# A four-layer hybrid backbone on one core: where the low halves of the weights are formed, and two edits in the Mamba-2 layer

## The chip, the cores and the metric

The kernel runs on one core of a Trainium2 chip. The metric is the device time of one execution, in microseconds (us), as the median of several runs. A core has TensorE (matmuls, "PE"; its weight loads are "PEld"), VectorE ("DVE"), ScalarE ("ACT"), GpSimd ("POOL") and SyncE ("SP"), which here only issues transfers. Each engine works through its own queue in order; the transfers (DMA) run beside them.

## The reference, cut to what matters

One inference step of a diffusion backbone: 128 context tokens and 512 latent tokens of width 1024 pass four layers, each with another token mixer: a bidirectional Mamba-2 SSD, a gated MLP, an S5 state-space layer with a GLU, and neighbourhood attention. Every layer projects into the mixer and out of it again:

```python
for i in range(DEPTH):                      # 4 layers
    hc, gate_c = adaln(xc, norm_g[i], cond_ctx @ w_mod[i] + b_mod[i])
    hl, gate_l = adaln(xl, norm_g[i], cond_lat @ w_mod[i] + b_mod[i])
    yc, yl = mixer_i(hc @ w_in), mixer_i(hl @ w_in)
    xc = xc + gate_c * (yc @ w_out[i])
    xl = xl + gate_l * (yl @ w_out[i])
```

In the SSD layer (32 heads in 8 groups of 4, chunks of 128 tokens) the result is the sum of a part within each chunk and a part from the state that enters the chunk, forward and backward:

```python
y_diag = einsum('bclgn,bcsgn,bgrcls,bcsgrp->bclgrp', cm, bm, decay_in, xd)
y_off  = einsum('bclgn,bcgrpn,bgrcl->bclgrp', cm, states, exp(a_cum))
y = y_diag + y_off
```

## The kernel before

The 640 tokens lie along the free axis, the channels on the 128 partitions. A big product runs as three matmuls of reduced-width fp32 (fp32r) pieces: each operand is split into a high half (`hi`, the value rounded) and a low half (`lo`, what rounding lost), and hi·hi + hi·lo + lo·hi is summed in PSUM. A *unit* is a weight block of 1024 x 128: it comes by one 512 KB transfer into a `raw` buffer (two of them), and `unit` makes `whi` and `wlo` of it (three buffers each). There are 289 units: 65 in the SSD layer with its output projection, 64 in the MLP layer, 80 in the S5 layer (32 in, 32 GLU, 16 out), 80 in the attention layer.

`unit` makes the halves so: ScalarE copies raw into `whi` (L223), ScalarE writes minus raw, rounded, into `wlo` (L224), and a transfer that GpSimd issues adds raw to `wlo` (L225). The raw buffer comes free when that transfer has ended. The older helper `split` (L201 to L204) instead subtracts hi from the source on an engine; `N.wlo` names that engine (VectorE, or GpSimd in the output projections and the attention layer), and `N.wlos` is a pattern of engines that the S5 layer sets and that `turn_over` clears. In the kernel before `unit` computes the engine and doesn't use it.

`stream` plays the units on TensorE in *slots*. A slot is one k-tile of one unit: 128 rows of the contraction, six matmuls of 320 columns. A unit is eight slots. While unit i - 1 has its first slot, unit i is made. Each layer gives `play` a table `at` of other work by slot. TensorE's order is written out by hand that way; in the SSD and the attention layer the order of the other engines and of SP's transfers is a planner's, in the S5 layer with its GLU those of VectorE, ScalarE and GpSimd are by hand too, as is the end of each output projection (from slot 112 on).

In the SSD layer each of the 8 groups has its table from a start slot t (52, 92, 132, 180, 228, ...): for the chunks, in the order 0, 1, 4, 2, 3 and 9 slots apart, `decay` (the matrix W by scans on VectorE), `turn` (transposes, products) and 9 slots later `diag` (the part of y within the chunk). The state goes through three steps j = 1 to 3: `fade` (GpSimd: H times a decay, into a new H buffer of three), `advance` (TensorE `st`, VectorE adds it to the new H) and 6 slots after it `off` (TensorE: H times C into PSUM; VectorE: times `eab`, which has a single buffer that `begin` fills for the next group; GpSimd or, in the last group, VectorE: added to y). `off` of j = 0 is at t + 7, of j = 1 to 3 at t + 24, t + 36 and t + 43. Four PSUM banks are shared by all of this. `diag` forms two products of 128 x 256, of which only the blocks of matching heads are used, and adds them to y in two steps of 64 partitions (L1061).

In the attention layer each pair of heads takes 32 slots for its weights q, k, v, z. `k` writes the split k into `K` by eight transfers from SP (L1965), and the first `scores` of the pair (L2048) reads it nine slots later. `scores` is followed by a softmax on VectorE and ScalarE (L2054 to L2059, L2059 scales e), and `turn` transposes e six slots later (L2071).

Of the kernel before, what the change touches and what calls it, by code (L numbers as in the profile page):

```python
# [9 lines left out]
AF = mybir.ActivationFunctionType  # L10
OP = mybir.AluOpType
# [19 lines left out]
TA, TY, TS, TG, TB = 6, 9, 6, 12, 6  # L31
# [86 lines left out]
class Net:  # L118
    def __init__(self, ctx, tc, I, O, layers):
        self.layers = layers  # L120
        self.ctx, self.tc, self.nc, self.I, self.O = ctx, tc, tc.nc, I, O
        nc = self.nc
        pool = lambda name, bufs=1, **k: ctx.enter_context(tc.tile_pool(name=name, bufs=bufs, **k))
        self.const = pool("const")
        self.ap = pool("act")
        self.wp = pool("wts")
        self.hp = pool("h")
        self.ps = pool("ps", space=PSUM)
        self.dr = pool("dr", space=DRAM)
        self.uid = 0  # L130
        c = self.const
        cm = c.tile([128, 136], F32, name="cmat")
        nc.sync.dma_start(cm, I["consts"][:, 0:136])
        self.ident = cm[:, 0:128]
        self.blk = cm[:, 128:136]
        self.ones = c.tile([128, 128], F32, name="ones")
        nc.vector.memset(self.ones, 1.0)
        self.eps = c.tile([128, 1], F32, name="eps")
        nc.vector.memset(self.eps, EPS)
        self.vec = c.tile([128, NVEC], F32, name="vec")  # L140
        nc.sync.dma_start(self.vec, I["vecs"])
        self.mods = {}
        self.beside = []
        self.late = []
        self.hs = []
        self.xd = I["x"]
        self.rest = False
        self.cut_in = None
        self.ready = []
        self.entry = {}  # L150
        self.nrow = NROW
        self.wlo = nc.vector
        self.wlos = ""


    def n(self, s):
# [60 lines left out]
    def unit(self, raw, m=128):  # L217
        hi, lo = (self.wp.tile([128, 8, m], F32R, tag=s, bufs=NHL, name=self.n(s)) for s in ("whi", "wlo"))
        e = self.wlo
        if self.wlos:  # L220
            e, self.wlos = {"p": self.nc.gpsimd, "v": self.nc.vector}[self.wlos[0]], self.wlos[1:] + self.wlos[0]
        nc = self.nc
        nc.scalar.copy(hi, raw)  # L223
        nc.scalar.activation(lo, raw, AF.Copy, scale=-1.0)  # L224
        nc.gpsimd.dma_start(lo, raw, accum_op=OP.add)  # L225
        return hi, lo

    def gemm(self, units, h, m=128):
# [490 lines left out]
    def put(self, yd, k, y):  # L719

        self.nc.sync.dma_start(yd[:, 2 * k:2 * k + 2, :], y)
# [62 lines left out]
class Ssd:  # L784
# [124 lines left out]
    def run(self, N, h):  # L909
        nc, I, tp = N.nc, N.I, N.tp  # L910
        self.pads = [tp.tile([128, 648], F32, name=f"pad{i}") for i in range(2)]
        self.pi = 0
        for t in self.pads:
            for a, b in ((0, 2), (130, 134), (646, 648)):
                nc.vector.memset(t[:, a:b], 0.0)
        W = I["w_ssd"]
        self.ssum = N.ssum()
        self.yd = N.dr.tile([128, 16, T], F32, name="yd0")
        N.put_beside()
        G = [{"g": g} for g in range(8)]  # L920
        jobs = []
        at = {}
        put = lambda s, f, *a: at.setdefault(s, []).append(lambda: f(*a))
        one = lambda w, f, *a: jobs.append(([W[w]], h, 128, lambda p: f(N, *a, p)))

        def tables(p):
            self.tab = self.tables(N, p)
        jobs.append(([I["w_dt"]], h, 64, tables))
        for s in range(5):
            put(TB * s + 8, lambda: next(self.tab))  # L930
        for g in range(8):
            for n, w in (("b", 32 + g), ("c", 40 + g), ("x0", 16 + 2 * g), ("x1", 17 + 2 * g)):
                one(w, self.conv, G[g], n, w - 16)
            for j in range(2 if g else 0):
                one(2 * g - 2 + j, self.gate, G[g - 1], j)

            t = 8 + 32 * (g + 1) + 16 * max(g - 1, 0) + TG + 8 * (g == 1)
            P = G[g]
            put(t - 2, self.begin, N, P)
            for i, c in enumerate((0, 1, 4, 2, 3)):  # L940
                put(t + TA * i - 8, self.decay, N, P, c)
                put(t + TA * i, self.turn, N, P, c)
                put(t + TA * i + TY, self.diag, N, P, c)
            put(t + 5, self.context, N, P)
            for j, s in enumerate((1, 2 * TA + TS, 4 * TA + TS, 4 * TA + 2 * TS + 1)):
                if j:
                    put(t + s - 3, self.fade, N, P, j)
                    put(t + s, self.advance, N, P, j)
                put(t + s + TS, self.off, N, P, j)
            for s in range(2):  # L950
                put(t + 16 * s, N.tick, 1)
        for j in range(2):
            one(14 + j, self.gate, G[7], j)
        N.play(jobs, at, after=[I["w_out"][0, 0, 0]])
        return self.yd, self.ssum
# [36 lines left out]
    def begin(self, N, P):  # L992

        nc, I, tp = N.nc, N.I, N.tp
        g = P["g"]
        P["H"] = self.t512(N, "H", 3)
        nc.sync.dma_start(P["H"], I["state_ssd"][:, g, :])
        P["eab"] = tp.tile([128, 2, 2, 512], F32, tag="eab", bufs=1, name=N.n("eab"))
        for k in range(2):
            nc.sync.dma_start(P["eab"][64 * k:64 * k + 64], self.ead[k, g][None].to_broadcast([64, 2, 2, 512]))  # L1000
# [48 lines left out]
    def diag(self, N, P, c):  # L1049

        nc = N.nc
        y, w = P["y"], P["W", c]
        py = N.bank("yd")
        for j in range(2):
            nc.tensor.matmul(py[:, 256 * j:256 * j + 256], P["xw", c][0][:, 128 * j:128 * j + 128], w[:, 256 * j:256 * j + 256],
                             start=True, stop=True)
        pv = py.rearrange("p (j h l) -> p j h l", j=2, h=2)
        for k in range(2):
            r = slice(64 * k, 64 * k + 64)
            o = y[r, :, 128 * c:128 * c + 128]  # L1060
            nc.vector.tensor_tensor(o, o, pv[r, :, k, :], op=OP.add)  # L1061

    def states(self, N, P, p, cf, cb):
        for d, c in ((0, cf), (1, cb)):
# [20 lines left out]
    def advance(self, N, P, j):  # L1085

        nc = N.nc
        Hn = P["Hn"]
        p = N.bank("st")
        self.states(N, P, p, j, 5 - j)  # L1090
        nc.vector.tensor_tensor(Hn, Hn, p, op=OP.add)
        P["H"] = Hn

    def off(self, N, P, j):

        nc = N.nc
        y, H = P["y"], P["H"]
        po = N.bank("off")
        for r in range(2):
            for d in range(2):  # L1100
                c = 1 + j if d == 0 else 4 - j
# [6 lines left out]
        for d in range(2):  # L1108
            c = 1 + j if d == 0 else 4 - j
# [472 lines left out]
class S5:  # L1582
# [80 lines left out]
    def turn_over(self, N, own, out):  # L1663
        own.close()
        out.enter_context(N.phase("glu"))
        N.nrow = 3
        N.wlos = ""

    def gate(self, N, k, p):
        z = self.tile(N, [128, T], "r3", 3)  # L1670
# [605 lines left out]
```

## Time and profile before

| | |
|---|---|
| time, median of 3 runs | 3116.27 us (3109.17 to 3117.82) |
| the profiled execution | 3107.51 us |
| its span, first to last instruction | 3105.7 us |
| TensorE busy, matmuls | 2776.5 us (89%) |
| VectorE, ScalarE, GpSimd busy | 1951.8 us (63%), 1595.9 us (51%), 1141.1 us (37%) |
| mean granted TensorE clock | 0.946 |
| transfers issued by SP, by GpSimd | 44.3% and 25.8% of 16 DMA engines' span |

The busy time tells which engine has little room; idle time of an engine that isn't the bound costs nothing. What sets the end is read from TensorE's idle time and from what ended each stretch of it. Layer by layer TensorE is in the SSD layer from about 60 us to 622, in its output projection to 760, in the MLP layer to 1340 with its output, in the S5 layer to 1885, the GLU to about 2140, its output projection to 2275, in the attention layer to 2950 and in the last projection to 3095.

### The profile page before, as it was taken

The page shows a single profiled execution, that of the slowest core. Times are in us where ns is not written, and L with a number is a line of the kernel's source. Part 1 is how long each engine was busy: PE and PEld are TensorE (multiplying, and loading weights), DVE is VectorE, ACT ScalarE, POOL GpSimd, SP SyncE. Part 2 cuts the span into 40 slices and gives each one's busy share as a digit, 9 for nine tenths or more (in the row PEclk, how much of TensorE's full clock was granted, in tenths as well). Part 3 has the DMA queues.
Part 4 walks back from the last instruction along what each step waited for, and adds up shares of the span by engine and source line. Part 5 has one row for each costly group of instructions (what it writes and reads, how often), then busy time and mean ns, then how long its engine had stood idle before and what let it go on. Part 6 is the DMA issues. An engine that isn't in the chain of part 4 may idle for free.

```text
span 3105.7 us, 50460 instructions
## 1 busy us (share of the span) xinstructions
PE 2776.5 (89%) x18252; PEld 2681.8 (86%) x18252; DVE 1951.8 (63%) x4958; ACT 1595.9 (51%) x2648; POOL 1141.1 (37%) x1482
## 2 busy tenths in 40 slices
PE   6888889899899998998889777998999999999988
PEld 3788889889899898988889777998989999999988
DVE  5987766675689888728887951006645656655732
ACT  4533444434444444265666454555356676666742
POOL 4467656412476672123453532332121111111110
PEclk8899999999999999999898898999999999999999
DMA  7666666687676677967767578667867766677575
GB/s 251 176 172 175 163 168 172 179 261 209 177 211 188 184 209 235 265 187 187 190 176 210 139 169 198 157 156 224 244 162 175 181 162 157 178 177 176 147 229 139
DMA packets 289736, 583.47 MB, mean 188 GB/s; under 512 B 79888, under 2 KB 148944, under 8 KB 288464
## 3 DMA queue, kind: packets, MB, share of 16 engines
q1 hardware_dynamic: 247424, 427.66, 44.3%
q0 software_dynamic: 42064, 152.59, 25.8%
q8 instruction: 145, 2.38, 0.3%
q14 instruction: 103, 0.84, 0.1%
HBM read 333.83 MB, written 65.70 MB: 129 GB/s over the span
## 4 chain that ended last, share of the span: by engine, by line
PE 33%; DMA 19%; DVE 12%; issue 8%; ACT 5%; POOL 3%; SPq 3%; POOLq 0%; DVEq 0%; ACTq 0%
PE acc L317 25%; DMA wlo<-raw 7%; DMA K<-k 3%; DVE S L1756 3%; DMA raw<-in_w_glu_dram 2%; DMA raw<-in_w_out_dram 2%; DVE sl L1753 2%; PE S L2048 1%; PE PT L2071 1%; SPq L1965 1%; ACT zr L1604 1%; SPq L1824 1%; PE av L2083 1%; ACT wlo L224 1%; ACT whi L223 1%
## 5 line engine op out<-in xcount | busy, mean ns | idle before, releaser
L317 PE MATMUL acc<-hhi,whi 128*128 128x320 f32 (+2 forms) x3472 | 865.9, 329 | 18.8 <-ACT hhi L203 8.5
L317 PE MATMUL acc<-hhi,wlo 128*128 128x320 f32 (+2 forms) x3472 | 827.9, 318 | 54.6 <-DMA wlo<-raw 54.1
L317 PE MATMUL acc<-hlo,whi 128*128 128x320 f32 (+2 forms) x3472 | 826.0, 317 | 3.2 <-DVE hlo L569 1.8
L225 POOL DMA_DIRECT2D wlo<-raw x289 | 253.8, 881 | 1135.1 <-ACT wlo L224 826.4
L317 PEld LDWEIGHTS acc<-hhi,wlo 128*128 128x128 f32 (+1 forms) x3472 | 600.9, 194 | 66.3 <-DMA wlo<-raw 64.8
L317 PEld LDWEIGHTS acc<-hhi,whi 128*128 128x128 f32 (+1 forms) x3472 | 602.9, 196 | 29.5 <-ACT hhi L203 14.0
L317 PEld LDWEIGHTS acc<-hlo,whi 128*128 128x128 f32 (+1 forms) x3472 | 605.0, 195 | 7.8 <-DVE hlo L569 4.2
L223 ACT CAST whi<-raw 128x1024 fp32r<-128x1024 f32 (+1 forms) x289 | 302.3, 1046 | 524.0 <-DMA raw<-in_w_out_dram 167.9
L224 ACT ACTIVATE wlo<-raw 128x1024 fp32r<-128x1024 f32 (+1 forms) x289 | 305.1, 1056 | 0.0
L429 DVE SCALAR_TENSOR_TENSOR wacc<-wm,conds,wacc 128x512 f32<-128x512 f32 x280 | 204.2, 787 | 21.6 <-DMA wm<-in_w_mod_dram 21.2
L317 PE MATMUL acc<-y,whi 128*128 128x320 f32 (+2 forms) x1024 | 203.0, 315 | 6.9 <-ACT y L203 3.4
L1756 DVE TENSOR_TENSOR S<-S,sl 128x32 f32<-128x32 f32 x1008 | 179.1, 232 | 0.0
L317 PEld LDWEIGHTS acc<-y,whi 128*128 128x128 f32 x1024 | 164.2, 191 | 10.7 <-ACT y L203 4.2
L1871 DVE TENSOR_TENSOR y<-y,sg 128x640 f32<-128x640 f32 x16 | 13.2, 825 | 202.5 <-ACT sg L1870 202.5
L905 DVE SCALAR_TENSOR_TENSOR cacc<-pad,vec,cacc 128x644 f32<-128x644 f32 x128 | 136.4, 1066 | 4.7 <-ACT cacc L903 3.0
L317 PE MATMUL acc<-y,wlo 128*128 128x320 f32 (+2 forms) x512 | 123.8, 313 | 11.2 <-DMA wlo<-raw 11.2
L2048 PE MATMUL S<-K,q 128*128 128x384 f32 (+1 forms) x320 | 91.2, 367 | 38.7 <-DMA K<-k 38.5
L2090 DVE TENSOR_TENSOR yn<-yn,av 64x128 f32<-64x128 f32 x320 | 90.4, 283 | 56.2 <-ACT yn L2088 48.5
L2007 POOL TENSOR_TENSOR yn<-yn,zn 128x128 f32<-128x128 f32 x80 | 36.5, 461 | 239.9 <-DVE yn L2090 123.5
L1753 DVE TENSOR_TENSOR sl<-S,A 128x64 f32<-128x64 f32 x504 | 119.3, 277 | 0.0
L1012 POOL TENSOR_TENSOR dd<-cmat,dt 128x512 f32<-128x512 f32 x80 | 107.7, 1353 | 15.3 <-DVE dt L816 9.7
L317 PE MATMUL acc<-gyh,wlo 128*128 128x320 f32 x384 | 94.6, 325 | 16.3 <-DMA wlo<-raw 16.3
(404 smaller groups left out, 5371.3 us busy)
## 6 DMA issues: line engine op xcount, KB each, us to landing
wlo<-raw POOLq DMA_DIRECT2D x288, 512.0 KB, 5.4
wm<-in_w_mod_dram SPq DMA_DIRECT2D x96, 512.0 KB, 6.5
raw<-in_w_out_dram SPq DMA_DIRECT2D x64, 512.0 KB, 3.9
raw<-in_w_nat_dram SPq DMA_DIRECT2D x64, 512.0 KB, 4.1
raw<-in_w_ssd_dram SPq DMA_DIRECT2D x48, 512.0 KB, 3.6
raw<-in_w_mlp_dram SPq DMA_DIRECT2D x48, 512.0 KB, 4.1
fb<-fd SPq DMA_DIRECT2D x40, 512.0 KB, 5.5
s5X<-s5gx SPq DMA_DIRECT2D x32, 512.0 KB, 5.5
```

The costliest lines, as they stand in the source:

```text
L223: nc.scalar.copy(hi, raw)
L224: nc.scalar.activation(lo, raw, AF.Copy, scale=-1.0)
L225: nc.gpsimd.dma_start(lo, raw, accum_op=OP.add)
L317: mm(p[:m, o:o + c], w[:, j, :], v(hx), start=(k == 0 and wi == 0), stop=(k == 8 * len(units) - 1 and wi == 2))
L429: e.scalar_tensor_tensor(acc[:, c], w[:, j], a, acc[:, c], op0=OP.mult, op1=OP.add)
L905: nc.vector.scalar_tensor_tensor(acc, pad[:, j:j + 644], w(j), acc, op0=OP.mult, op1=OP.add)
L1012: nc.gpsimd.tensor_tensor(dg.rearrange("p (h l) -> p h l", h=4), N.ident[:, None, :].to_broadcast([128, 4, 128]), self.dt[:, c, 32 * d + 4 ...
L1753: e.tensor_tensor(t[d], F[:, d, at[d], None, :].to_broadcast([128, 2, 32]), A[:, :, d], op=OP.mult)
L1756: e.tensor_tensor(dst[d], dst[d], t[d][:, k].rearrange("p (r g) -> p r g", r=2)[:, ::1 - 2 * k], op=OP.add)
L2007: N.nc.gpsimd.tensor_tensor(y[:, o], y[:, o], P["z"][:, o], op=OP.mult)
L2048: nc.tensor.matmul(p[:, :n], P["q"][:, hh, 128 * b:128 * b + 128], K[:, hh, i, c:c + n], start=(i == 0), stop=(i == 1))
L2090: nc.vector.tensor_tensor(y[r, o], y[r, o], p[r, w:w + 128], op=OP.add)
```

## The change

Three edits. First, `unit` has two ways. With `adds` true (the start) it forms the low half by the adding transfer as before, but in another order: negation, transfer, then the copy into `whi`. With `adds` false it calls `split`, and the engine that `N.wlo` names subtracts. `turn_over`, played at slot 270 of the S5 layer, sets `adds` false, so the units made from then on (most of the GLU's, the third output projection, the attention layer and the last projection) are split by subtraction: 30 on VectorE and 95 on GpSimd; 164 stay with the transfer. Second, `off` of j = 1 to 3 stands four slots later, and it reads the state kept for its own j. Third, `diag` forms its part of y by heads, in four products of 64 x 128 that land on the partitions where y has that head, and adds all with one step.

```diff
     def unit(self, raw, m=128):
-        nc.scalar.copy(hi, raw)
-        nc.scalar.activation(lo, raw, AF.Copy, scale=-1.0)
-        nc.gpsimd.dma_start(lo, raw, accum_op=OP.add)
+        if self.adds:
+
+            self.nc.scalar.activation(lo, raw, AF.Copy, scale=-1.0)
+            self.nc.gpsimd.dma_start(lo, raw, accum_op=OP.add)
+            self.nc.scalar.copy(hi, raw)
+        else:
+            self.split(raw, hi, lo, lo_eng=e)
         return hi, lo
...
-                put(t + s + TS, self.off, N, P, j)
+                put(t + s + TS + (4 if j else 0), self.off, N, P, j)
...
     def diag(self, N, P, c):
         py = N.bank("yd")
+
         for j in range(2):
-            nc.tensor.matmul(py[:, 256 * j:256 * j + 256], P["xw", c][0][:, 128 * j:128 * j + 128], w[:, 256 * j:256 * j + 256],
-                             start=True, stop=True)
-        pv = py.rearrange("p (j h l) -> p j h l", j=2, h=2)
-        for k in range(2):
-            r = slice(64 * k, 64 * k + 64)
-            o = y[r, :, 128 * c:128 * c + 128]
-            nc.vector.tensor_tensor(o, o, pv[r, :, k, :], op=OP.add)
+            for k in range(2):
+                h = 2 * j + k
+                nc.tensor.matmul(py[64 * k:64 * k + 64, 128 * j:128 * j + 128], P["xw", c][0][:, 64 * h:64 * h + 64],
+                                 w[:, 128 * h:128 * h + 128], start=True, stop=True)
+        o = y[:, :, 128 * c:128 * c + 128]
+        nc.vector.tensor_tensor(o, o, py[:, 0:256].rearrange("p (j l) -> p j l", j=2), op=OP.add)
...
-        P["H"] = Hn
+        P["H"] = P["H", j] = Hn
...
-        y, H = P["y"], P["H"]
+        y, H = P["y"], P["H", j]
...
         N.wlos = ""
+        N.adds = False
```

## Rows read from the trace of the kernel before

**Rows 1.** Windows: start:end, us, busy of PE, PEld, DVE, ACT, POOL; PEclk, DMA, GB/s.

```profile
55.00:622.00 567.00, 491.13 (x3108) 473.85 (x3109) 419.44 (x509) 246.58 (x391) 328.90 (x268) 0.93 0.68 173
...
2275.00:2950.00 675.00, 630.96 (x4276) 622.47 (x4275) 406.44 (x1362) 464.81 (x1023) 129.60 (x214) 0.96 0.69 172
```

**Rows 2.** Waits of TensorE over the span: waiting line, releaser, us, times, longest.

```profile
PE acc L317 <- DMA wlo<-raw: 88.1, 48, 8.6
PE off L1102 <- DVE H L1091: 43.1, 13, 6.1
PE S L2048 <- DMA K<-k: 38.5, 15, 4.1
```

**Rows 3.** Timeline of TensorE, SSD layer: start, us, line, operands, records [idle before].

```profile
189.21 2.04 PE L1102 MATMUL off<-c,H 128*128 128x128 f32 x8 [6.07 <-DVE H L1091]
192.65 1.91 PE L1067 MATMUL st<-xw,xb 128*128 128x256 f32 x4
...
301.33 0.46 PE L317 MATMUL acc<-hhi,whi 128*128 128x320 f32 x2
...
302.21 0.46 PE L317 MATMUL acc<-hhi,whi 128*128 128x320 f32 x2
...
438.69 1.13 PE L1102 MATMUL off<-c,H 128*128 128x128 f32 x8 [2.96 <-DVE H L1091]
440.54 1.02 PE L1067 MATMUL st<-xw,xb 128*128 128x256 f32 x4
```

**Rows 4.** The instructions of diag: duration ns min/median/max, first and last start, shape.

```profile
L1055 PE MATMUL yd<-dd,xb x160: 378/379/634, 136.1 to 625.1; 128*128 128x256 f32 x160
L1061 DVE TENSOR_TENSOR y<-y,yd x80: 383/419/426, 142.2 to 626.0; 64x256 f32<-64x256 f32 x80
```

**Rows 5.** Waits of TensorE for low halves: 760:1200, 1885:2140, 2140:2280, 2950:3095, in order.

```profile
PE acc L317 <- DMA wlo<-raw: 26.6, 17, 4.2
...
PE acc L317 <- DMA wlo<-raw: 16.6, 15, 1.3
...
PE acc L317 <- DMA wlo<-raw: 6.6, 2, 6.4
...
PE acc L317 <- DMA wlo<-raw: 5.3, 1, 5.3
```

**Rows 6.** Negation (ns min/median/max), and transfers: count, KB, us to landing.

```profile
L224 ACT ACTIVATE wlo<-raw x289: 625/1055/1084, 41.0 to 3068.8; 128x1024 fp32r<-128x1024 f32 x144, 128x512 fp32r<-128x512 f32 x1
...
wlo<-raw POOLq DMA_DIRECT2D x288, 512.0 KB, 5.4
...
eab<-ead SPq DMA_DIRECT2D x16, 512.0 KB, 6.5
```

**Rows 7.** Timelines of SP's queue and of TensorE, attention layer.

```profile
2382.94 0.33 SPq L214 DMA_DIRECT2D raw<-in_w_nat_dram  x1
...
2384.33 8.51 SPq L1965 DMA_DIRECT2D K<-k  x8
...
2393.46 0.48 PE L2048 MATMUL S<-K,q 128*128 128x256 f32 x2 [2.52 <-DMA K<-k]
...
2561.73 0.77 PE L2048 MATMUL S<-K,q 128*128 128x256 f32 x2 [3.81 <-DMA K<-k]
```

**Rows 8.** Groups by form, GpSimd: shape, count, busy us, mean ns, idle before.

```profile
L204 POOL TENSOR_TENSOR K<-ckv,K 128x256 fp32r<-128x256 f32 x16 | 11.7, 731 | 24.4 <-ACT K L203 24.4
...
L204 POOL TENSOR_TENSOR vT<-ckv,vT 128x128 fp32r<-128x128 f32 x16 | 7.4, 461 | 72.2 <-ACT vT L203 72.2
```

**Rows 9.** Timelines of VectorE, GpSimd and TensorE, attention layer.

```profile
2596.75 0.41 DVE L2059 TENSOR_SCALAR e<-e,mx 128x384 f32<-128x384 f32 x1
...
2599.66 0.49 PE L2071 MATMUL PT<-cmat,e 128*128 128x128 f32 x3
...
2892.67 0.73 POOL L204 TENSOR_TENSOR K<-ckv,K 128x256 fp32r<-128x256 f32 x1 [3.56 <-ACT K L203]
...
2892.72 0.90 DVE L2059 TENSOR_SCALAR e<-e,mx 128x384 f32<-128x384 f32 x1
```

More of the change, by code (lines that the diff above doesn't have):

```diff
@@ L153, in __init__ @@
         self.wlos = ""
+        self.adds = True
     def n(self, s):
@@ L221, in unit @@
             e, self.wlos = {"p": self.nc.gpsimd, "v": self.nc.vector}[self.wlos[0]], self.wlos[1:] + self.wlos[0]
-        nc = self.nc
-        nc.scalar.copy(hi, raw)
-        nc.scalar.activation(lo, raw, AF.Copy, scale=-1.0)
-        nc.gpsimd.dma_start(lo, raw, accum_op=OP.add)
+        if self.adds:
[4 more added lines that the diff above has]
+            self.split(raw, hi, lo, lo_eng=e)
         return hi, lo
@@ L995, in begin @@
         g = P["g"]
-        P["H"] = self.t512(N, "H", 3)
+        P["H"] = P["H", 0] = self.t512(N, "H", 3)
         nc.sync.dma_start(P["H"], I["state_ssd"][:, g, :])
```

## The prediction, made before the changed kernel was run

> **What bounds the kernel now.** Three views, in this order. The busy time by stretch says which engine each layer leans on: in the first layer TensorE is busy 491 of 567 us, VectorE 419 and GpSimd 329; in the attention layer TensorE is busy 631 of 675, VectorE 406 and GpSimd only 130 [rows 1]. So TensorE is the bound and only its idle time counts: VectorE, the next, still has a quarter of the first layer free. TensorE's waits, summed, then say what ends that idle time: 88.1 us in 48 waits for the low half of a weight, 43.1 us in 13 waits of an `off` matmul for the state H, 38.5 us in 15 waits of the attention scores for the transfers of K [rows 2]. The three make 170 us, and the change touches all three. The timeline last, for what stands around one wait. It also shows a price beyond the wait itself: after the 6.07 us wait at 189.21 the same `off` group took 2.04 us and its successor 1.91, where after the 2.96 us wait at 438.69 they took 1.13 and 1.02 [rows 3]. There TensorE ran at the lower of its two clock levels, 1.2 instead of 2.4 GHz (granted over the layer: 0.93 [rows 1]). From `off` to `st` it cost 3.44 against 1.85 us, and 0.9 more in `st`: 2.5 us a spell. The sum is made against the profiled execution: 3105.7 us of span, 3107.5 us in all, 8.8 below the median of the runs (3116.3). I take the sum off 3107.5 and add the 8.8 at the end.
>
> **Part 1: `off` of j = 1 to 3 four slots later.** A slot is one k-tile of the weight stream: three pairs of matmuls, 301.33 to 302.21, 0.88 us [rows 3]. Four slots are 3.52 us of TensorE work put between advance (where VectorE gets its sums) and the matmul that reads H. A wait shrinks by up to that. Ten of the 13 vanish; the three above 3.52 (6.07, the first of them [rows 3], 5.17 and 4.93) leave 2.55, 1.65 and 1.41. So 43.1 - 5.6 = 37.5 us. Five `off` groups took 2.04 or 2.05 us as that at 189.21 did; five spells at 2.5 give 12.5. Together 50. Against it: H now sits on VectorE behind its convolutions, and a TensorE that no longer waits gets ahead, so H, the weights W or a free one of the four PSUM banks are late next. Also, `eab` has one buffer: its reload waits for `off`(3), and lands 6.5 us after its issue [rows 6]. In the first two groups `off`(3) and the next group's `off`(0) now fall into one slot (52 + 47 = 92 + 7), where four lay between; the sum of that `off`(0) holds a bank for as long. Bounds 0 and 2 x 6.5 = 13. SP is held by that reload too, 3.5 us longer, with raw weight loads behind it; with the transfers at 0.68 of their time [rows 1] and 567 us for 49 weights I cost that at nothing, and at the same 13 if the cover is gone. I take 8 off: **42**, bounds 10 and 50.
>
> **Part 2: y by heads.** Two matmuls of 256 columns become four of 128 columns and 64 output rows. In the trace an fp32 matmul is two records; 40 chunks give 160 records of 256 columns [rows 4], afterwards 320 of 128. Eight records of 128 columns (`off`, 438.69) are no longer than four of 256, so in a row the four cost about the same; 0.1 us more a chunk if the gaps open gives +4 us. VectorE loses 40 of 80 additions of 0.42 us [rows 4], 17 us off its queue and not on TensorE's path. The trace has no two matmuls on the two halves of the output rows. If halves ran side by side, 0.43 of 0.85 us a chunk would go, 17 us. I take **0**, by the row nearest in shape, ends +4 and -17. The Trainium skill, "TensorEngine Tiling (Array Packing)", section "Tiling Modes", says that tiles of 64 columns load and multiply in parallel, and that changing the mode drains the engine. No row of this kernel shows either; by the first half alone the sum would be 17 better.
>
> **Part 3: the low half first, where transfers still add** (164 of 289 weights). Negation and copy on ScalarE swap. The negation takes 1.05 us, the transfer 5.4 from its issue [rows 6]; the low half comes 1.05 sooner, the copy 1.05 later, and the copy is needed some 0.6 us ahead of it but is ready about 4 earlier, so the transfer covers it. TensorE waits in these layers 88.1 - 16.6 - 6.6 - 5.3 = 59.6 us in 30 waits; 17 of them, 26.6 us, in the second layer [rows 5]. Cutting each by at most 1.05 gives 27 of the 59.6. Some of it moves to whatever is next late: **16**, bounds -10 (the copy slips behind other work of ScalarE) and 30. GpSimd waits 1.05 less at each issue, and everything queued there gains.
>
> **Part 4: 125 weights by subtraction.** `turn_over` is played at slot 270, when weight 34 has been made: 30 subtractions on VectorE in the GLU, 95 on GpSimd after it. Gone are a negation on ScalarE, an issue and 5.4 us of transfer each; raw is released at the end of the subtraction. Price on GpSimd: 0.46 us for 128 columns and 0.73 for 256, so 2.1 ns a column and 2.34 us for 1024 [rows 8]. From raw's copy the low half needs 2.34 instead of 1.05 + 5.4 = 6.45 us, 4.1 sooner. That covers all 15 waits of the GLU (16.6 us, none over 1.3), and 4.1 each of the 6.4 and 5.3 us at the two later ones [rows 5]: 24.8. Both are as long as that at 189.21 nearly, so I count a slow spell for each: +5. **29**, bounds 16 and 33. Behind a waiting subtraction on GpSimd stand the gates of yn and the splits of the cached keys; the issue it replaces waited longer there, for the negation.
>
> **Part 5: K.** K's first transfer left at 2384.33, right behind a raw load that SP had held until 2382.94 for a low half's transfer; K's eight took 8.51 us to issue, and the scores began at 2393.46, 2.52 late [rows 7]. An earlier release sends the raw load before that, and no 512 KB addition competes. The first is worth about 1 us a pair, the second is open. The wait is 38.5 / 15 = 2.6 a pair; about five pairs also have a slow spell as at 2561.73 (0.77 against 0.48 us) [rows 7]: 10 more. Bounds 0 (the planner orders SP so that the raw load still goes first) and 48. I take **28**.
>
> **Part 6: the new work on GpSimd.** About 63 subtractions of 2.34 us in the attention layer, less as many issues, raise GpSimd from 130 to some 220 of 675 us. They can hold up VectorE. At 2892.67 GpSimd's split ran 0.73 us, and VectorE's scaling of e, begun at 2892.72, took 0.90 instead of 0.41 to 0.42 [rows 9]. It waited for GpSimd's end. The scaling at 2596.75 ended 2.5 us ahead of its transposition at 2599.66 [rows 9]. So a hold of up to 2.34 is just covered; without that cover 63 x a fifth x 1.2 us = 15. I take **-5**, bounds -20 and 0. The Trainium skill, "SBUF — State Buffer", section "Who interferes with whom", states such a rule: whoever is first keeps the shared ports for a whole instruction. The trace agrees (0.90 against 0.42).
>
> **Sum.** 42 + 0 + 16 + 29 + 28 - 5 = 110. 3107.5 - 110 = 2997.5, and 8.8 more: **3006 us**.
>
> **Rivals.** *K stays late.* SP is ordered by a planner; if the raw load still leaves right before K, or K's eight issues are the limit, part 5 gives nothing: 3034. For it: the eight issues alone fill 8.5 us. Against: the raw load did wait for a transfer that is gone. *The wait for H only moves.* If the planner puts H correspondingly later on VectorE, or TensorE waits for banks, part 1 gives 10: 3038. For it: VectorE is busy 74% there. Against: H has a fixed place behind work that TensorE's slots pace. With both, 3066. *The low half doesn't come sooner*, since planned work gets between: part 3 gives nothing, 3022, inside the range. *Slower: GpSimd holds VectorE where TensorE needs it.* The 95 subtractions, mostly in the attention softmax, hold scalings and the splits behind them; at a full 2.34 us each on TensorE's path 222 us are lost against 42 + 16 + 29 = 87 gained without K: 3251. It is slower than before from 87 / 95 = 0.92 us a subtraction on. Against it: 2.5 us of slack. *Better.* The two halves of y run side by side and K's waits and all spells go: 17 + 20 more, 2969.
>
> **How the numbers follow.** Forecast (2985 to 3030) 0.47; K late 0.17; H only moves 0.11; both 0.06; better 0.09; GpSimd in the way 0.10. The likeliest is 3006. The range reaches from below the better case, with all upper bounds, to beyond both shortfalls together: 2955 to 3080; about 0.1 is left out above and 0.05 below. About 0.3% is what a measurement of this kernel can tell from no change. Faster 0.88; same 0.04 (a third of both shortfalls, a fifth of the GpSimd case); slower 0.08, the rest of that case.
>
> **What would show it.** Right: the wait of `off` for H under 10 us; no wait for a low half's transfer after some 1900 us of the before's time; raw loads in the attention layer no longer held by such a transfer; the scores' wait for K under 15 us; 95 subtractions at 2.3 to 2.5 us on GpSimd and 30 on VectorE; 40 additions of y. Wrong: a new large wait of transpositions for e or pt, `off` waiting as before, K's wait unchanged.

## The result, and the profile of the changed kernel

| | before | after |
|---|---|---|
| median | 3116.65 us (3109.17 to 3117.82) | 3027.93 us (3021.86 to 3036.23) |
| ratio after / before, 95% interval | | 0.9733 (0.971 to 0.9757) |
| profiled execution: time, span | 3107.51, 3105.7 us | 3021.86, 3020.1 us |
| mean granted clock of TensorE | 0.946 | 0.954 |

The change makes the kernel 2.7% faster: 88.7 us between the medians, 85.7 between the profiled executions. The forecast was 110 us and 3006; the time lies in its range, 22 us above it. The sum came out nearly right, its terms did not: by themselves one is about a fifth of what was forecast, one is nothing, and one is larger by two fifths.

Where the gain lies is read from when TensorE first and last uses low halves of each kind of weight (`y`: first and last projection, `yhi`: the second projection, `gyh`: the GLU and the third projection, `hhi`: the four layers' own). Up to the first projection 16.1 us are gained (625.9 to 609.8), up to the end of the second layer's projection 21.7 in all, up to the first weight of the GLU 20.9. GLU and third projection bring it to 36.5 (2273.7 to 2237.2), the attention layer to 80.8 (2961.6 to 2880.8), the last projection to 85.9. So the attention layer alone gives 44.3 us, the first layer 16.1, GLU and third projection 15.6. These compare one execution of each kernel. Among the other kernels of this study, code that is unchanged in the attention layer took 674.7 to 688.1 us there (687.9 before) and the change's own 643.3 to 645.6 (643.6 after); for GLU and third projection it is 383.5 to 390.1 and 362.0 to 369.8. The attention layer's gain is thus 29 to 45 us, that of GLU and third projection 14 to 28.

TensorE's waits over the span, of after: waiting line, releaser, us in total, times, longest. They answer to [rows 2].

```profile
PE acc L321 <- DMA wlo<-raw: 43.2, 25, 6.6
...
PE off L1106 <- DVE H L1095: 3.4, 7, 0.6
...
PE S L2053 <- DMA K<-k: 2.0, 1, 2.0
```

All three waits fell, by 121 us together, and the time fell by 86. The rest went into other waits. Most stand in the first layer; the same view of after, 38 to 606 us:

```profile
PE st L1071 <- DVE xw L1041: 12.3, 5, 3.3
PE xbT L1037 <- ACT x L910: 9.5, 6, 1.9
PE stc L1071 <- DVE xw L1041: 9.2, 3, 6.7
...
PE st L1071 <- DVE off L1110: 5.7, 2, 2.9
PE G L1048 <- DVE y L1065: 3.7, 1, 3.7
PE xbT L1037 <- DVE dd L1051: 3.5, 2, 1.9
```

These six add up to 43.9 us; in the kernel before the same six add up to 4.5. The operations themselves, after, against [rows 4], [rows 6] and [rows 8]: name and operands, count, ns min/median/max or busy us and mean ns.

```profile
L1065 DVE TENSOR_TENSOR y<-y,yd x40: 387/407/422, 142.9 to 610.3; 128x256 f32<-128x256 f32 x40
...
L205 POOL TENSOR_TENSOR wlo<-raw,whi 128x1024 fp32r<-128x1024 f32 x95 | 244.8, 2578 | 308.9 <-ACT whi L204 295.8 <-DVE mx L2061 7.7 <-POOL vT L205 3.1
...
L205 DVE TENSOR_TENSOR wlo<-raw,whi 128x1024 fp32r<-128x1024 f32 x30 | 35.5, 1221 | 0.6
```

Counts are as forecast (40 additions of y, 95 subtractions on GpSimd, 30 on VectorE), and a GpSimd subtraction has a mean of 2.58 us against an estimate of 2.34.

### The profile page after: what moved, and what is told of

The parts are those of the page before. It is cut to its first block, busy times and chain, and to the rows that moved or that the text cites. A ratio compares the mean times of both kernels' runs of the same rounds, so it can differ in the third digit from the quotient of the medians.

```text
span 3020.1 us, 50547 instructions
## 1 busy us (share of the span) xinstructions
PE 2750.9 (91%) x18412; PEld 2643.5 (88%) x18412; DVE 2051.4 (68%) x4948; ACT 1472.4 (49%) x2523; POOL 1265.0 (42%) x1452
## 5 line engine op out<-in xcount | busy, mean ns | idle before, releaser
L321 PE MATMUL acc<-hhi,wlo 128*128 128x320 f32 (+2 forms) x3472 | 824.2, 317 | 37.7 <-DMA wlo<-raw 36.4
L205 POOL TENSOR_TENSOR wlo<-raw,whi 128x1024 fp32r<-128x1024 f32 x95 | 244.8, 2578 | 308.9 <-ACT whi L204 295.8
L226 POOL DMA_DIRECT2D wlo<-raw x164 | 145.9, 895 | 540.4 <-ACT wlo L225 497.8
L227 ACT CAST whi<-raw 128x1024 fp32r<-128x1024 f32 (+1 forms) x164 | 170.4, 1039 | 227.5 <-DMA raw<-in_w_mlp_dram 75.4
L225 ACT ACTIVATE wlo<-raw 128x1024 fp32r<-128x1024 f32 (+1 forms) x164 | 173.0, 1056 | 143.0 <-DMA raw<-in_w_mlp_dram 80.9
L433 DVE SCALAR_TENSOR_TENSOR wacc<-wm,conds,wacc 128x512 f32<-128x512 f32 x280 | 222.6, 849 | 19.5 <-DMA wm<-in_w_mod_dram 19.3
L204 ACT CAST whi<-raw 128x1024 fp32r<-128x1024 f32 x125 | 129.4, 1048 | 107.4 <-PE acc L321 84.2
L1761 DVE TENSOR_TENSOR S<-S,sl 128x32 f32<-128x32 f32 x1008 | 171.3, 224 | 0.0
L909 DVE SCALAR_TENSOR_TENSOR cacc<-pad,vec,cacc 128x644 f32<-128x644 f32 x128 | 154.6, 1208 | 3.8 <-ACT cacc L907 2.0
L2062 ACT ACTIVATE e<-sb,mx 128x384 f32<-128x384 f32 x128 | 78.9, 617 | 96.8 <-DVE mx L2061 94.9
L1758 DVE TENSOR_TENSOR sl<-S,A 128x64 f32<-128x64 f32 x504 | 125.9, 290 | 0.0
```

Of the source, the lines that this page charges most:

```text
L204: (hi_eng or nc.scalar.copy)(hi, src)
L205: (lo_eng or nc.vector).tensor_tensor(lo, src, f(hi), op=OP.subtract)
L225: self.nc.scalar.activation(lo, raw, AF.Copy, scale=-1.0)
L226: self.nc.gpsimd.dma_start(lo, raw, accum_op=OP.add)
L227: self.nc.scalar.copy(hi, raw)
L321: mm(p[:m, o:o + c], w[:, j, :], v(hx), start=(k == 0 and wi == 0), stop=(k == 8 * len(units) - 1 and wi == 2))
```

## The experiments

Gains in us below are what the ratio lacks to 1, times 3111 us, the median of the kernel before in the first set.

**The parts one by one, each put alone into the kernel before.** First, `off` later:

```diff
-                put(t + s + TS, self.off, N, P, j)
+                put(t + s + TS + (4 if j else 0), self.off, N, P, j)
```

(with `P["H", j]` kept as in the change.)

> The kernel before with one edit: off of j = 1 to 3 four slots later, with the state that it reads kept by its number. The forecast's part 1: 42 us off (bounds 10 and 50), so a ratio of about 0.9865; the wait of off for H under 10 us. Rival, the wait only moves: about 10 us off, ratio 0.997, with new waits of st and stc for xw and of the transposition for x and dd that add up to 25 us or more in the first layer.

Measured: 3104.74 us, ratio 0.9972 (0.995 to 0.9995), 9 us off (2 to 16). The rival holds by its time; the waits that it named (`st` and `stc` for xw, the transposition for x and dd) add up to 15.3 us, against 4.5 before, and not to 25. TensorE's waits in the first layer, this kernel:

```profile
PE xbT L1033 <- ACT x L906: 8.3, 6, 1.6
PE acc L317 <- ACT pad L900: 7.0, 4, 1.8
PE yd L1055 <- DVE y L1061: 6.0, 4, 2.2
...
PE G L1044 <- DVE xw L1037: 4.8, 2, 3.9
PE G L1044 <- DVE y L1061: 4.5, 1, 4.5
PE stc L1067 <- DVE xw L1037: 3.6, 2, 2.7
PE off L1102 <- DVE y L1061: 3.5, 1, 3.5
...
PE off L1102 <- DVE H L1091: 3.0, 3, 1.0
```

The wait for H fell from 43.1 to 3.0 us, and 37.7 us stand in the other seven lines, where the kernel before has 7.4: TensorE waits for the same VectorE and ScalarE at another instruction.

Second, `diag` as in the change, alone:

> The kernel before with one edit: a chunk's y by heads on their own partitions. The forecast's part 2: no change (ends +4 and -17), ratio 1.000; the 17 us taken off VectorE's queue bring nothing. Rival one, the halves overlap: 17 us of TensorE's time go, ratio 0.9945. Rival two, VectorE's shorter queue is what counts: H comes some 0.8 us sooner a chunk, the 13 waits for H shrink by 10 us or more and the ratio is 0.996 or lower without any gain in the matmuls.

Measured: 3120.96 us, ratio 1.002 (0.9998 to 1.0042), 6 us lost (1 gained to 13 lost). The forecast's zero holds; neither rival does. The wait for H is still 40.9 us in 14 times, and a new one of `st` for `xw` is 9.6.

Third, the order of negation and copy, alone and only where transfers still add in the change (`adds` is cleared as there):

```diff
-        nc.scalar.copy(hi, raw)
         nc.scalar.activation(lo, raw, AF.Copy, scale=-1.0)
         nc.gpsimd.dma_start(lo, raw, accum_op=OP.add)
+        nc.scalar.copy(hi, raw)
```

> The kernel before with one edit: the low half's negation and adding transfer ahead of the high half's copy, for the 164 weights of the first three layers and the leaves between them; the other weights as before. The forecast's part 3: 16 us off (bounds -10 and 30), ratio 0.995. Rival, the low half hardly comes sooner (in the changed kernel the second layer still waits 24.6 us for it, against 26.6 before): 0 to 4 us off, ratio 0.999 to 1.000.

Measured: 3113.89 us, ratio 1.0001 (0.9982 to 1.0021): nothing in the time. In the first layer the waits for low halves do fall, from 15.0 us in 4 to 6.4 in 1, but others grow by as much (of `stc` for xw from 1.2 to 6.2, of `yd` for y from 2.9 to 6.1), and the layer ends no sooner (626.7 against 625.9). In the second layer the low halves come no sooner. The timelines of ScalarE, GpSimd and TensorE show why at one weight of the second layer, before:

```profile
844.96 1.05 ACT L224 ACTIVATE wlo<-raw 128x1024 fp32r<-128x1024 f32 x1
...
846.69 0.29 POOL L1489 TENSOR_TENSOR Qt<-s5qw,s5cw 128x32 f32<-128x32 f32 x1
846.91 0.89 POOL L225 DMA_DIRECT2D wlo<-raw  x1
...
851.50 0.90 PE L317 MATMUL acc<-hhi,wlo 128*128 128x320 f32 x2 [3.77 <-DMA wlo<-raw]
```

and the same weight with the order swapped:

```profile
845.41 1.06 ACT L225 ACTIVATE wlo<-raw 128x1024 fp32r<-128x1024 f32 x1 [2.50 <-DMA raw<-in_w_mlp_dram]
...
848.19 0.29 POOL L1495 TENSOR_TENSOR Qt<-s5qw,s5cw 128x32 f32<-128x32 f32 x1
848.41 0.89 POOL L226 DMA_DIRECT2D wlo<-raw  x1
...
852.89 0.90 PE L323 MATMUL acc<-hhi,wlo 128*128 128x320 f32 x2 [3.77 <-DMA wlo<-raw]
```

Before, the negation ended at 846.01 and the transfer was issued at 846.91, 0.9 us later; now it ends at 846.47, right after raw's landing, and the issue comes at 848.41, 1.94 later. GpSimd issues the transfers in the order of its own queue, and ahead of this one stand its table operations, back to back. The microsecond won on ScalarE is lost there, and TensorE's wait is 3.77 us in both. Of the 17 transfers that TensorE waits for in the second layer before [rows 5], GpSimd stood idle for the negation ahead of only one.

Fourth, the subtraction, alone (`adds` is cleared by `turn_over` as in the change):

```diff
+        if self.adds:
             nc.scalar.copy(hi, raw)
             nc.scalar.activation(lo, raw, AF.Copy, scale=-1.0)
             nc.gpsimd.dma_start(lo, raw, accum_op=OP.add)
+        else:
+            self.split(raw, hi, lo, lo_eng=e)
```

> The kernel before with one edit: from the turn to the GLU on, 125 low halves by a subtraction (30 on VectorE, 95 on GpSimd) and no adding transfer. The forecast's parts 4 to 6: 29 + 28 - 5 = 52 us off, ratio 0.983. Rival, K's waits and the spells after them go nearly whole (the changed kernel has 2.0 us of them left): 65 to 75 us off, ratio 0.976 to 0.979. If the parts are independent, the four single edits of this set add up to about 89 us.

Measured: 3044.75 us, ratio 0.9763 (0.9726 to 0.98), 74 us off (62 to 85). The rival holds: more than the forecast's 52. Its attention layer takes 643.3 us (2250.5 to 2893.8), as in the changed kernel (643.6), so the other parts do nothing there.

The four single edits add up to 9 - 6 + 0 + 74 = 77 us, the change gives 83 by its ratio (76 to 90). The difference is within the intervals, but the profiles show a place for it. First use of the first projection's low half, in the kernels before, with `off` later, with y by heads, and after, in this order:

```profile
L317 PE MATMUL acc<-y,wlo x512: 279/309/635, 625.9 to 3091.1; 128*128 128x320 f32 x160, 128*128 128x256 f32 x6, 128*128 128x384 f32 x5
...
L317 PE MATMUL acc<-y,wlo x512: 279/309/636, 618.3 to 3082.1; 128*128 128x320 f32 x160, 128*128 128x256 f32 x6, 128*128 128x384 f32 x5
...
L317 PE MATMUL acc<-y,wlo x512: 279/309/636, 630.3 to 3108.0; 128*128 128x320 f32 x160, 128*128 128x256 f32 x6, 128*128 128x384 f32 x5
...
L321 PE MATMUL acc<-y,wlo x512: 279/309/468, 609.8 to 3005.2; 128*128 128x320 f32 x160, 128*128 128x256 f32 x6, 128*128 128x384 f32 x5
```

Alone, `off` ends the layer 7.6 us sooner and y by heads 4.4 later; together (with the swapped order) it is 16.1 sooner, and every later kernel of this study that has them lies between 607 and 610. With `off` later TensorE waits 14.0 us for VectorE's additions of y (the three lines of y above: 6.0, 4.5, 3.5); after, with half as many additions, 4.0 (3.7 for `G`, 0.3 for `yd`). So y by heads may pay once the wait for H is out of the way. But the swapped order may, too: TensorE's waits for low halves in the first layer are 15.8 us with `off` later and 7.9 after, a fall as large as the 8.5 us by which the layer ends sooner (618.3 to 609.8). Which of the two it was is not shown; no kernel with `off` later and just one of them was run.

**The halves of y.** In the kernel after, the four matmuls in another order:

```diff
-        for j in range(2):
-            for k in range(2):
+        for k in range(2):
+            for j in range(2):
```

> The kernel after, but the four matmuls of a chunk's y in another order: both of the upper 64 output rows, then both of the lower. Read from the trace, not from the time. In the kernel after, the eight records of a chunk take 0.58 us from their first start to the next matmul's, where off's eight of the same columns take 0.81; the starts around them are 0.39 apart where 0.29 is usual. Theory, neighbours on different halves overlap in part, and the change of shape costs 0.1 on each side: with this order the group goes to 0.65 us or more (only one of three neighbouring pairs is on different halves) and the 0.39 stay. Rival, 64 columns are simply quicker to load: the group stays at 0.58.

Measured by the timeline of TensorE around one chunk (the kernel's one run took 3026.94 us). Before:

```profile
284.70 0.46 PE L317 MATMUL acc<-hhi,wlo 128*128 128x320 f32 x2
284.99 1.03 PE L1055 MATMUL yd<-dd,xb 128*128 128x256 f32 x4
285.67 0.64 PE L317 MATMUL acc<-hhi,whi 128*128 128x320 f32 x2
286.15 0.46 PE L317 MATMUL acc<-hlo,whi 128*128 128x320 f32 x2
```

After, the halves in turn:

```profile
303.43 0.46 PE L321 MATMUL acc<-hhi,wlo 128*128 128x320 f32 x2
303.82 0.66 PE L1062 MATMUL yd<-dd,xb 128*64 128x128 f32 x8
304.40 0.56 PE L321 MATMUL acc<-hhi,whi 128*128 128x320 f32 x2
304.80 0.45 PE L321 MATMUL acc<-hlo,whi 128*128 128x320 f32 x2
```

One half after the other:

```profile
301.97 0.46 PE L321 MATMUL acc<-hhi,wlo 128*128 128x320 f32 x2
302.36 0.66 PE L1062 MATMUL yd<-dd,xb 128*64 128x128 f32 x8
302.95 0.56 PE L321 MATMUL acc<-hhi,whi 128*128 128x320 f32 x2
303.35 0.31 PE L321 MATMUL acc<-hlo,whi 128*128 128x320 f32 x1
```

From the start ahead of the chunk to the second start behind it: 1.45 us before, 1.37 after, 1.38 in the other order. The eight records take 0.58 and 0.59 us, so it is not the overlap of neighbours on different halves that makes them shorter than `off`'s eight (0.81, 311.52 to 312.33 in the kernel after); the rival fits. The loads of 64 columns have a median of 137 ns, those of 128 columns before 190. Whether that is the whole cause is not shown. And the start ahead of the group is 0.39 away where it was 0.29. Net 0.08 us a chunk, 3 us over 40; the other chunks have the same figures (1.45, 1.37 and 1.38 in the middle).

**What made K late.** Two kernels put back into the attention layer of the kernel after one thing each that the adding transfer had brought. The bytes (`extra`, a tile in memory, is there only for the attention layer):

```diff
+            if self.extra is not None:
+                self.nc.gpsimd.dma_start(self.extra, hi)
```

> The kernel after, but in the attention layer each subtraction is followed by a transfer of the high half (512 KB) to memory on GpSimd's queue: the bytes of the adding transfer are back, raw is released as in the kernel after. Theory, SP's hold made K late: the scores' wait for K stays under 10 us, ratio 0.972 to 0.977. Rival, the traffic did: the wait for K comes back (25 us or more), ratio 0.980 to 0.987.

Measured: 3047.46 us, ratio 0.9791 (0.9758 to 0.9824); the wait for K is 11.4 us in 10 times. Neither as stated: the ratio lies between the two ranges, and the wait came back only in part. The bytes cost 16.1 us in this layer (below), but they are not the adding transfer's whole load. Transfers of GpSimd's queue from 2240 to 2870 us, before and here (packets, MB, share of 16 engines):

```profile
q0 software_dynamic: 8566, 31.16, 27.1%
...
q0 software_dynamic: 8640, 31.46, 13.6%
```

As plain transfers to memory the same bytes take half the share. And raw held longer:

```diff
+            if self.extra is not None:
+                self.nc.gpsimd.dma_start(self.extra, raw[:, 0, 0:8])
```

> The kernel after, but in the attention layer each subtraction is followed by a transfer of 4 KB that reads raw, on GpSimd's queue: raw is released only when it lands, some 2 us after the subtraction, and next to no traffic is added. Theory, K was late because SP stood behind a raw buffer that was still held: the scores' wait for K comes back (25 us or more) and 20 to 40 us of the gain go, ratio 0.980 to 0.987. Rival, it was the traffic of the adding transfers: the wait for K stays under 8 us, ratio 0.972 to 0.976.

Measured: 3031.36 us, ratio 0.9738 (0.9706 to 0.977), wait for K 2.1 us. It decides nothing: the small transfer needs only raw and was placed ahead of the subtraction (2303.38 against 2305.79 in GpSimd's timeline), so nothing was held. The same flaw is in the next, meant to bring both:

```diff
+            if self.extra is not None:
+                self.nc.gpsimd.dma_start(self.extra, raw)
```

> The kernel after, but in the attention layer each subtraction is followed by a transfer of the whole of raw (512 KB) to memory: the bytes are back and raw is held until they have landed, some 6 us. A hold of 2 us alone cost nothing (wait for K 2.1 us), the bytes alone 11.4 us of wait and 18 us of time. Theory, the two act together (a raw load that stands in SP's queue ahead of K, and slow transfers): the wait for K rises to 25 us or more and the ratio to 0.984 or more. Rival, the bytes are all of it: wait for K 9 to 14 us, ratio 0.977 to 0.981, and what else the attention layer gained is not K's.

Measured: 3033.4 us, ratio 0.9752 (0.9722 to 0.9782), wait for K 3.6 us in 1 time. Neither. These transfers, too, left ahead of the subtraction, once raw had landed (2308.29, the subtraction 2310.78). In this example one left 6.3 us ahead of K (2314.63), and they land in 3.4 us in the middle; the next left at 2317.17, while SP issued K. In the kernel with the bytes of the high half one left at 2318.65, 1.5 us ahead of K (2320.16). So as many bytes at other moments cost 3.6 us of wait for K in place of 11.4. A hold that does hold:

```diff
+            if self.extra is not None:
+                self.pcopy(raw[:, 0, 0:8], f(lo[:, 0, 0:8]))
+                self.nc.gpsimd.dma_start(self.extra, raw[:, 0, 0:8])
```

> The kernel after, but in the attention layer GpSimd, once it has subtracted, overwrites eight columns of raw out of the low half and sends just these (4 KB) to memory: raw can't be released before the subtraction has ended and the transfer landed, some 3 us later than in the kernel after. (The earlier attempt at a hold held nothing: its transfer left ahead of the subtraction.) Theory, SP standing behind a held raw makes K late: SP's waits ahead of its raw loads, 28 ns at most in the kernel after and 2 us in the middle, 9 at most, in the kernel before, are back, the wait for K is 10 us or more, and 10 to 25 us go: ratio 0.977 to 0.981. Rival, only the bytes in flight beside K matter (11.4 us of wait and 18 us of time by themselves): the wait for K stays under 5 us, ratio 0.972 to 0.976, whatever SP waits.

Measured: 3026.34 us, ratio 0.9725 (0.9694 to 0.9756), wait for K 1.2 us. SP's waits ahead of its raw loads in the attention layer (ns min/median/max) before, after and here:

```profile
L214 SPq EVENT_SEMAPHORE  x80: 17/1965/8985, 2275.3 to 2944.4; - x80
...
L215 SPq EVENT_SEMAPHORE  x63: 17/17/28, 2244.9 to 2863.6; - x63
...
L216 SPq EVENT_SEMAPHORE  x94: 17/28/10288, 2249.1 to 2870.0; - x94
```

They are back only in part (median 28 ns, longest 10.3 us), for the planner saw the hold and put the raw load behind K: SP issues K at 2309.05 and raw at 2316.01, where the kernel after issues raw at 2381.21 ahead of K at 2382.68. So a held raw does not make K late where the order can still be chosen; whether it did in the kernel before, where raw stood ahead of K [rows 7], wasn't tried.

The layer as a whole, from the last low half of the third projection to the layer's own last, for before, the kernel with `off` later (in this layer the code of before), after, bytes, hold, and the subtraction on VectorE (next): us, TensorE's busy time, granted clock, DMA share.

```profile
2273.70:2961.60 687.90, 643.55 (x4366) 0.96 0.69 172
...
2278.30:2953.00 674.70, 631.02 (x4366) 0.98 0.71 176
...
2237.20:2880.80 643.60, 626.46 (x4366) 0.99 0.47 133
...
2250.00:2909.70 659.70, 631.92 (x4365) 0.99 0.64 180
...
2241.90:2886.20 644.30, 627.51 (x4365) 0.99 0.45 134
...
2250.50:2878.20 627.70, 622.22 (x4366) 1.00 0.48 137
```

Of the 44.3 us, 27.2 are idle time of TensorE (44.35 to 17.14) and 17.1 busy time: the same matmuls, at a granted clock of 0.99 in place of 0.96. Only the idle time is firm. In the three single edits that leave this layer as before it is 43.7 to 47.8 us, but their busy time is 631.0 to 642.8 at a granted clock of 0.97 to 0.98: of the 17.1 us, about 5 stand outside what the same code shows from one execution to the next. The bytes bring 16.1 us back, the hold 0.7. The remaining 28 of the 44, or 14 against the fastest of the three, are not reproduced by either.

**GpSimd in VectorE's way.** The attention layer's 63 subtractions on VectorE:

```diff
-        N.wlo = N.nc.gpsimd
+        N.wlo = N.nc.vector
```

> The kernel after, but in the attention layer the subtractions are VectorE's (1.22 us each) and not GpSimd's (2.58 us). Theory of the slower rival, GpSimd's subtractions hold VectorE's work: without them the 8.7 us in which the transpositions wait for e go and the time falls by 5 to 10 us, ratio 0.970. Rival, VectorE is the engine that the softmax needs (441 of 633 us busy, and 77 more by this): the waits for e and for pt grow to 20 us or more and the time rises by 10 to 25 us, ratio 0.976 to 0.981.

Measured: 3009.67 us, ratio 0.9672 (0.9641 to 0.9702): about 19 us below the kernel after, more than the theory had. VectorE's scaling of e (busy us, mean ns), before, after and here:

```profile
L2059 DVE TENSOR_SCALAR e<-e,mx 128x384 f32<-128x384 f32 x128 | 55.2, 431 | 3.7
...
L2064 DVE TENSOR_SCALAR e<-e,mx 128x384 f32<-128x384 f32 x128 | 90.9, 710 | 3.2
...
L2064 DVE TENSOR_SCALAR e<-e,mx 128x384 f32<-128x384 f32 x128 | 55.2, 431 | 3.1
```

and one of the held ones in the kernel after, GpSimd's subtraction beside it:

```profile
2300.01 2.41 POOL L205 TENSOR_TENSOR wlo<-raw,whi 128x1024 fp32r<-128x1024 f32 x1
...
2300.96 1.67 DVE L2064 TENSOR_SCALAR e<-e,mx 128x384 f32<-128x384 f32 x1
```

The scaling ends at 2302.63, the subtraction at 2302.42. Of the 128 scalings in the kernel after, 33 overlap a subtraction and take 1.65 us in the middle, the other 95 take 0.42. Of TensorE's waits, the 8.7 us of the transpositions for e are gone; for a low half from GpSimd it had waited only once, 1.3 us, so it is not the length of the subtractions that held it. The last step moves the leaves' subtractions as well (32 by the trace, not the 62 that the expectation names), `self.wlo = nc.vector` in the leave:

> The kernel after, but all 125 subtractions on VectorE, in the last two leaves too (62 there and in between were GpSimd's beside the 63 of the attention layer's weights). Theory, GpSimd's subtractions hold VectorE wherever both work: the 8.2 us in which the third leave's matmuls wait for VectorE's x go as well, and the time is 3 to 10 us below that of the kernel with the attention's 63 alone on VectorE: ratio 0.964 to 0.966. Rival, VectorE has enough to do in the leaves (112 of 135 us busy) and low halves come late there: ratio 0.968 to 0.972.

Measured: 2995.91 us, ratio 0.9634 (0.96 to 0.9669), the theory. The wait of the third projection's matmuls for `x` fell from 8.2 to 0.8 us, which it was in the kernel before. This kernel beats both: 3.7% below the kernel before, some 1% below the change.

Last, the third layer's weights by subtraction too:

```diff
-        N.wlos = WLO5
+        N.adds = False
```

> As the kernel with all subtractions on VectorE, and the weights of the third layer too (no adding transfer from there on). Theory, bytes cost time wherever transfers of the layer's own are waited for: the third layer's waits for its transposition tables (20 us) halve, its clock rises from 0.91, and 10 to 20 us go: ratio 0.958 to 0.962. Rival, VectorE's 383 of 547 us there and its order leave no room: waits for a low half on VectorE and for VectorE's tables grow by as much, ratio 0.964 to 0.970.

Measured: 2987.14 us, ratio 0.9606 (0.9571 to 0.9642). The ratio lies in the theory's range, but the interval reaches over the one above, and the waits speak for the rival: 21.0 us of `mT` and 13.7 of `y` for VectorE's `r`. From the second projection's last low half to the GLU's first it takes 547 us, in the kernel above 552. The lowest time of the study, but that this last step helps is not shown.

## Why the prediction was right, and where its sum was not

**The direction and the bounds of the kernel: right.** TensorE's idle time was the place to look, of the three waits of [rows 2] two went nearly whole and the third halved, and no new wait is as large as the smallest of them.

**Part 1 (42 us, lower bound 10): wrong.** Alone it gave 9 (2 to 16), about its lower bound. The step that failed is "a wait shrinks by up to that": four slots between advance and `off` do take the wait of `off` for H away, but TensorE, no longer held, comes to the next product of VectorE or ScalarE as much sooner and waits there. The 74% busy VectorE [rows 1] was read as a reserve, where it stands in a chain within each group. The rival "the wait for H only moves" gave 10 us and named this; it had a chance of 0.11 and should have had most of it. The slow spells did not go either: the layer's granted clock is 0.94 against 0.93. The sign that the prediction named for this part, a wait of `off` for H under 10 us, came (3.4): one wait that falls doesn't tell that time is saved.

**Part 2 (0): right alone, by luck in part.** The row taken as the nearest was misread: from its start to the next matmul's, `off`'s group at 438.69 takes 0.89 us (next start 439.58) and the four of 256 columns at 440.54 take 0.67 (441.21), so by that row a chunk would have become dearer. That eight records with 64 output rows take only 0.58 us made up for it: a chunk costs 1.37 in place of 1.45 us on TensorE. In the overlap case, too, a chunk's four take 0.68 us (284.99 to 285.67), not 0.85. The 17 us saved on VectorE are worth nothing while `off` waits for H; once it doesn't, they or the swapped order, or both, are worth some 9 us. That pairing was not foreseen.

**Part 3 (16 us): nothing alone.** The step that failed is that the low half comes 1.05 us sooner if its negation does. In the second layer the transfer waits for its turn on GpSimd, not for the negation; in the first the waits shrink, and others take their place while `off` waits for H. GpSimd is busy 329 of 567 us in the first layer [rows 1] and 286 of 443 in the second, and the timeline of GpSimd around one late transfer would have shown its table work; it was not read. The second layer's waits in the kernel after (744 to 1182) are 24.6 us in 17 against 26.6 in 17 [rows 5].

**Parts 4 to 6 (29 + 28 - 5 = 52 us): 74 measured; gain and price both undersized.** With the subtractions on VectorE the ratio is 0.9634 against 0.9733: 31 us lie in the choice of GpSimd. So the gain without its subtractions would be about 105 where 57 was forecast, and these cost 31 where 5 was forecast (bounds 0 and 20). GLU and third projection came in at 15.6 us against 16.6 + 6.6 of waits in [rows 5], with 8.2 lost to the wait for x there. The attention layer is where the size was off: part 5 took 28 us, spells included, and the wait for K alone went from 38.5 to 2.0. TensorE's busy time fell on top, by 17.1 us against the kernel before and by 4.6 against the fastest execution of the same code; part 5 had counted 10 for spells.

**The slower rival** had its mechanism right and its price wrong. 31 us over 95 subtractions are 0.33 us each, against 0.92 from which it would have decided. "A hold of up to 2.34 is just covered" was nearly so: 13 waits for e, at most 0.7 us. But the scalings, 279 ns longer in the mean, add 36 us to VectorE: part 6 put a hold without cover at a fifth of 63 subtractions and 1.2 us each, and 33 scalings were held by 1.23 us in the middle. The Trainium skill, "SBUF — State Buffer", section "Who interferes with whom", states the lock; the trace agrees (0.71 against 0.43 us in the mean).

**Part 5's reasons:** that bytes beside K matter is shown: they bring 9.4 of the 36.5 us of wait back (2.0 to 11.4), with half the adding transfers' share of the DMA engines. That SP's hold behind raw mattered is not shown, nor excluded. The remaining 27 us of wait stay open between the rest of that load, the hold in the old order and the slower issue: K's eight took 8.51 us before, 5.80 at 2382.68 after, 5.96 at 2320.16 with the bytes of the high half, and 7.15 at 2314.63 with those of raw, where a transfer left in their midst.

The errors offset each other: of the 110 us, 33 too much stood in part 1, 16 in part 3 and 26 in the price of GpSimd's hold, against some 48 too little for the transfers that are gone; 83 are left, as the ratio has it, if part 2 counts at nothing. That the sum holds is luck in part. A forecast that holds by its sum can still be wrong in most of its terms.

## What to carry to other kernels

A wait of the bounding engine for a chain on another is not taken away by moving its reader back: ask what the next reader of the same engine is, and count only what the slower chain leaves over. Before an edit brings a transfer's input sooner, look whether the queue that issues it is free at that moment. And when a transfer is replaced by an operation, try it on each engine that could do it: here 1.22 us on VectorE, with 441 of 633 us busy, were better than 2.4 us on GpSimd with 226, for GpSimd's work also stretches VectorE's.

## What the runs showed of the hardware that was not expected

- A GpSimd subtraction of 2.4 us stretched VectorE scalings from 0.41 up to 1.67 us and the mean of 128 from 431 to 710 ns. The other way round it is read from a timeline only: GpSimd's own subtractions, 2.41 us in the middle, took up to 8.34 in the third projection, and the longest, at 2144.46, ran while VectorE worked without a gap.
- Eight fp32 records with 64 output rows took 0.58 us, and 0.59 with the halves in the other order; `off`'s eight with 128 rows took 0.81. The Trainium skill, "TensorEngine Tiling (Array Packing)", section "Tiling Modes", says that changing the mode drains the engine; 0.10 us more ahead of each group fits that. Its parallel tiles no order here brought out.
- VectorE's convolutions in the first layer went from a mean of 1066 ns to 1135 with y by heads alone and 1208 in the kernel after: 18 us more on 128 of them, as much as the halved additions of y saved. Which engine stretches them was not tried.
- Adding transfers between tiles, 31.16 MB of them, took 27.1% of the 16 DMA engines' span in the attention layer; plain transfers of 31.46 MB from a tile to memory took 13.6%.
